# RMSNorm and QKV product on one core: the head of the kernel rewritten as a list schedule, with x tiles first, single weight blocks, and one PSUM pool

## The chip, the cores and the metric

One core of a Trainium2 chip (trn2). The metric is the device time of one execution in microseconds (us); several executions of each kernel are taken and the median is quoted. The profile's span runs from the first to the last instruction and is about 1.8 us shorter than the time. Times inside a profile are counted from the start of the span.

"PE" is the matrix engine, "PEld" its weight loads, "DVE" VectorE, "ACT" ScalarE, "POOL" GpSimd; "SPq" is the queue from which nearly all transfers are issued. In this kernel PE writes its results to tiles in PSUM (eight banks), and VectorE or ScalarE copies them out. A "K block" is 128 of the 768 rows of the weights, and a "unit" is one tile of x times 512 (at the end 256) weight columns.

## The reference

```python
# x: (8, 1024, 768) f32, gamma: (768,), w_qkv: (768, 2304) f32, eps = 1e-5
rms = np.sqrt(np.mean(x ** 2, axis=-1, keepdims=True) + eps)
return np.matmul(x / rms * gamma, w_qkv).astype(np.float32)
```

## The kernel before

The 8192 rows are 64 tiles of 128 rows. A tile of x is transposed (K to the partitions), multiplied with the weights in bf16 (6 K blocks, 4.5 units of 512 columns), and scaled by 1/rms when it is copied out of PSUM. Gamma goes into the weights as they are cast to bf16. The weights are needed whole by every tile and take 7.1 MB, so the kernel begins with a "head": six tiles of x are worked on while the weights arrive in pieces. The 58 other tiles come after it, one after another, and are transposed by transfers instead of by PE.

The order of arrival (w is the next weight piece, x the next tile), and the pieces (first and last K block, first column, columns):

```python
ARRIVALS = "wxxxwxwwxwxww"
PIECES = [(0, 3, 0, 512), (3, 6, 0, 512), (0, 3, 512, 512), (3, 6, 512, 512),
          (0, 6, 1024, 512), (0, 6, 1536, 512), (0, 6, 2048, 256)]
EARLY = 3        # x tiles transposed by PE in f32
FIRST_XBAR = 6   # from this tile on: transposed by a transfer
WARM = 7
...
    psum_t = ctx.enter_context(tc.tile_pool(name="psum_t", bufs=2, space=bass.MemoryType.PSUM))
    psum_mm = ctx.enter_context(tc.tile_pool(name="psum_mm", bufs=6, space=bass.MemoryType.PSUM))
```

Every operation is given a planned time with `at`; at the end the plan is sorted by it and issued. The times only fix the order on each engine; each engine then runs its own list strictly in that order and waits where it must. In the head a simple rule makes the plan: a clock `now` advances with each arrival, casts go to an engine by K block, and each new piece is multiplied with all tiles there are (shortened; the loads, and four more warm-up matmuls behind the transposes of x0, are left out).

```python
    def conv_w(c):
        k0, k1, n0, n = PIECES[c]
        for ko in range(k0, k1):
            ...
            if ko % 3 == 0:   # VectorE   o = i * g
            elif ko % 3 == 1: # ScalarE
            else:             # GpSimd

    at(0.0, idle, WARM)       # matmuls on zeros: keep PE busy
    at(3.0, gamma_in)
    at(3.1, idle, WARM)
    for n, kind in enumerate(ARRIVALS):
        if kind == "x":
            now += 1.02
            if t < EARLY:
                at(now, trans_f32, t); at(now + 0.6, copy_f32, t); ready = now + 1.2
            else:
                at(now, cast_x, t); at(now + 0.6, trans_pe, t); at(now + 1.0, copy_xT, t); ready = now + 1.7
            at(now + 0.7, stat, t)      # ScalarE: sum of squares, root
            at(now + 1.6, recip, t)     # VectorE: waits for stat
            for c in ws: unit(...)      # products with all pieces there are
        else:
            at(now, conv_w, c)
            for t in xs: unit(...)
    for t in range(HEAD, MT):           # the 58 tiles after the head
        at(T - 15, load_x, t); at(T - 8.5, cast_x, t); at(T - 7.5, trans_dma, t)
        at(T - 5, stat, t); at(T - 3, recip, t)
        ...
```

Of the kernel before, what the change touches and what calls it, by code (L numbers as in the profile page):

```python
# [7 lines left out]



ARRIVALS = "wxxxwxwwxwxww"
PIECES = [(0, 3, 0, 512), (3, 6, 0, 512), (0, 3, 512, 512), (3, 6, 512, 512),
          (0, 6, 1024, 512), (0, 6, 1536, 512), (0, 6, 2048, 256)]

EARLY = 3

FIRST_XBAR = 6
WARM = 7


@with_exitstack
def kernel(
# [8 lines left out]
    nc = tc.nc  # L31
    f32 = mybir.dt.float32
    bf16 = mybir.dt.bfloat16
    AF = mybir.ActivationFunctionType
    mult = mybir.AluOpType.mult
# [4 lines left out]
    Kw, N = w_qkv.shape  # L40
    assert K == Kw
    P = 128
    KO = K // P
    MT = M // P
    NT = 512
    HEAD = ARRIVALS.count("x")
    inv_k = 1.0 / float(K)
    PIECE_BUFS = {(k1 - k0, n): sum((q[1] - q[0], q[3]) == (k1 - k0, n) for q in PIECES)
                  for k0, k1, _, n in PIECES}

    PARTS = [(0, 1024), (1024, 1024), (2048, N - 2048)]

    singles = ctx.enter_context(tc.tile_pool(name="singles", bufs=1))
# [4 lines left out]
    xbp = ctx.enter_context(tc.tile_pool(name="xbp", bufs=4))  # L58
    xTp = ctx.enter_context(tc.tile_pool(name="xTp", bufs=HEAD + 3))
    outp = ctx.enter_context(tc.tile_pool(name="outp", bufs=7))  # L60
    psum_t = ctx.enter_context(tc.tile_pool(name="psum_t", bufs=2, space=bass.MemoryType.PSUM))
    psum_mm = ctx.enter_context(tc.tile_pool(name="psum_mm", bufs=6, space=bass.MemoryType.PSUM))

    ctx.enter_context(tc.manual_schedule())

    g6 = singles.tile([KO, P], f32)
    nc.scalar.dma_start(out=g6, in_=gamma.rearrange("(ko p) -> ko p", p=P))
    eps_sb = singles.tile([P, 1], f32)
    nc.vector.memset(eps_sb, float(eps))  # L69
    warm = singles.tile([P, NT], bf16)  # L70
    nc.vector.memset(warm, 0.0)  # L71

    tbl = singles.tile([P, 1], f32)
    nc.scalar.activation(out=tbl, in_=eps_sb, func=AF.Sqrt)  # L74
    ident_f = singles.tile([P, P], f32)
# [3 lines left out]
    g_sb = singles.tile([P, KO], f32)  # L79
    w_b = singles.tile([P, KO, N], bf16)  # L80
    wv = w_qkv.rearrange("(ko p) n -> p ko n", p=P)

    X, XB, XT, RS, OUT, WF, PM, PT = {}, {}, {}, {}, {}, {}, {}, {}
# [5 lines left out]
    def load_w(c):  # L89
        k0, k1, n0, n = PIECES[c]  # L90
        WF[c] = wst.tile([P, k1 - k0, n], f32, name=f"w_f{k1 - k0}_{n}", bufs=PIECE_BUFS[k1 - k0, n])
        nc.sync.dma_start(out=WF[c], in_=wv[:, k0:k1, n0:n0 + n])

    def conv_w(c):
        k0, k1, n0, n = PIECES[c]
        for ko in range(k0, k1):
            o, i, g = w_b[:, ko, n0:n0 + n], WF[c][:, ko - k0, :], g_sb[:, ko:ko + 1]
            if ko % 3 == 0:
                nc.vector.tensor_scalar(out=o, in0=i, scalar1=g, scalar2=None, op0=mult)  # L99
            elif ko % 3 == 1:  # L100
                nc.scalar.activation(out=o, in_=i, func=AF.Copy, scale=g, bias=0.0)  # L101
            else:
                nc.gpsimd.tensor_scalar(out=o, in0=i, scalar1=g, scalar2=1.0, op0=mult, op1=mult)  # L103

    def cast_x(t):
        XB[t] = xbp.tile([P, K], bf16, name="xb")
        nc.vector.tensor_copy(out=XB[t], in_=X[t])  # L107

    def stat(t):
        sq = junk.tile([P, K], bf16, name="sq")  # L110
# [8 lines left out]
        nc.vector.reciprocal(out=r, in_=RS[t])  # L119
        RS[t] = r  # L120

    def trans_pe(t):
        PT[t] = psum_t.tile([P, KO, P], bf16, name="pt")
        for ko in range(KO):
            nc.tensor.transpose(out=PT[t][:, ko, :], in_=XB[t][:, ko * P:(ko + 1) * P], identity=ident)  # L125

    def copy_xT(t):
        XT[t] = xTp.tile([P, KO, P], bf16, name="xT")
        nc.vector.tensor_copy(out=XT[t], in_=PT[t])  # L129

    KA = 4

    def trans_f32(t):
        PT[t] = (psum_t.tile([P, KA, P], f32, name="pt"), psum_t.tile([P, KO - KA, P], f32, name="pt"))
        for ko in range(KO):
            o = PT[t][0][:, ko, :] if ko < KA else PT[t][1][:, ko - KA, :]
            nc.tensor.transpose(out=o, in_=X[t][:, ko * P:(ko + 1) * P], identity=ident_f)  # L137

    def copy_f32(t):
        XT[t] = xTp.tile([P, KO, P], bf16, name="xT")  # L140
        nc.vector.tensor_copy(out=XT[t][:, :KA, :], in_=PT[t][0])  # L141
        nc.scalar.copy(out=XT[t][:, KA:, :], in_=PT[t][1])  # L142

    def trans_dma(t):
        XT[t] = xTp.tile([P, KO, P], bf16, name="xT")
        nc.sync.dma_start_transpose(out=XT[t], in_=XB[t])

    def mm(t, n0, nl, k0=0, k1=KO):
        if k0 == 0:
            PM[t, n0] = psum_mm.tile([P, NT], f32, name="pm")  # L150
        for ko in range(k0, k1):
            nc.tensor.matmul(out=PM[t, n0][:, :nl], lhsT=XT[t][:, ko, :], rhs=w_b[:, ko, n0:n0 + nl],  # L152
                             start=(ko == 0), stop=(ko == KO - 1))

    def part(n0):
        return max(i for i, (p0, _) in enumerate(PARTS) if p0 <= n0)

    def evac(t, n0, nl, on_dve):
        h = part(n0)
        if (t, h) not in OUT:  # L160
            OUT[t, h] = outp.tile([P, PARTS[h][1]], f32, name=f"ot{h}")
        o = OUT[t, h][:, n0 - PARTS[h][0]:n0 - PARTS[h][0] + nl]
        pm = PM[t, n0]
        if on_dve:
            nc.vector.tensor_scalar(out=o, in0=pm[:, :nl], scalar1=RS[t], scalar2=None, op0=mult)  # L165
        else:
            nc.scalar.activation(out=o, in_=pm[:, :nl], func=AF.Copy, scale=RS[t], bias=0.0)  # L167
# [9 lines left out]
    def at(time, fn, *args):  # L177
        plan.append((time, len(plan), fn, args))

    def gamma_in():  # L180
        g_ps = psum_t.tile([P, KO], f32, name="pt")
        nc.tensor.transpose(out=g_ps, in_=g6, identity=ident_f[:KO, :KO])  # L182
        nc.vector.tensor_copy(out=g_sb, in_=g_ps)

    US = 6 * 0.2158 / 512
    left = {}
    state = {"pe": 0.0, "flip": 0}

    def unit(t, n0, nl, ready=0.0, k0=0, k1=KO):
        s = max(state["pe"], ready)  # L190
        state["pe"] = e = s + nl * US * (k1 - k0) / KO
        at(s, mm, t, n0, nl, k0, k1)
        if k1 < KO:
            return
        state["flip"] ^= 1
        at(e + 0.2, evac, t, n0, nl, state["flip"])
        h = part(n0)
        left[t, h] = left.get((t, h), PARTS[h][1]) - nl
        if t == MT - 1:
            at(e + 0.9, store, t, h, n0, nl)  # L200
        elif left[t, h] == 0:
            at(e + 1.4, store, t, h, *PARTS[h])

    def idle(n):
        wps = psum_mm.tile([P, NT], f32, name="pm")
        for _ in range(n):
            nc.tensor.matmul(out=wps, lhsT=warm[:, :P], rhs=warm, start=True, stop=True)  # L207

    at(0.0, idle, WARM)
    at(3.0, gamma_in)  # L210
    at(3.1, idle, WARM)
    now, xs, ws = 2.75, [], []
    for n, kind in enumerate(ARRIVALS):
        if kind == "x":
            t = len(xs)
            at(0.1 * n - 9, load_x, t)
            now += 1.02
            if t < EARLY:
                at(now, trans_f32, t)
                at(now + 0.6, copy_f32, t)  # L220
                if t == 0:
                    at(now + 0.1, idle, 4)
                ready = now + 1.2
            else:
                at(now, cast_x, t)
                at(now + 0.6, trans_pe, t)
                at(now + 1.0, copy_xT, t)
                ready = now + 1.7
            at(now + 0.7, stat, t)
            at(now + 1.6, recip, t)  # L230
            xs.append(t)
            for c in ws:
                k0, k1, n0, nl = PIECES[c]
                unit(t, n0, nl, ready, k0, k1)
        else:
            c = len(ws)
            k0, k1, n0, nl = PIECES[c]
            at(0.1 * n - 9, load_w, c)
            now += (k1 - k0) * nl * 4.1 / (KO * 512)
            at(now, conv_w, c)  # L240
            ws.append(c)
            for t in xs:
                unit(t, n0, nl, now + 0.9, k0, k1)

    n_tiles = [(i, min(NT, N - i)) for i in range(0, N, NT)]
    for t in range(HEAD, MT):
        T = state["pe"]
        at(T - 15, load_x, t)
        if t < FIRST_XBAR:
            at(T - 4.5, cast_x, t)  # L250
            at(T - 3.0, trans_pe, t)
            at(T - 2.5, copy_xT, t)
        else:
            at(T - 8.5, cast_x, t)
            at(T - 7.5, trans_dma, t)
        at(T - 5, stat, t)
        at(T - 3, recip, t)
        for n0, nl in n_tiles:
            unit(t, n0, nl)

    for _, _, fn, args in sorted(plan, key=lambda p: p[:2]):
        fn(*args)
# [35 lines left out]
```

## Time and profile before

| | |
|---|---|
| time, median of 3 runs | 391.52 us |
| span of the profiled run (a run of 392.31 us) | 390.5 us |
| busy: PE, ACT, DVE, POOL | 98%, 47%, 39%, 2% |
| first product of the head | 9.46 us |
| last copy of the head's outputs | 47.89 us |
| last copy of all | 386.89 us |

Read the order of time as: start, length, engine, line of the kernel, operation, output<-inputs, how many; in brackets how long the engine was idle just before, and what ended that.

### The profile page before, as it was taken

The page shows a single profiled execution, that of the slowest core. Times are in us where ns is not written, and L with a number is a line of the kernel's source. Part 1 is how long each engine was busy: PE and PEld are TensorE (multiplying, and loading weights), DVE is VectorE, ACT ScalarE, POOL GpSimd, SP SyncE. Part 2 cuts the span into 40 slices and gives each one's busy share as a digit, 9 for nine tenths or more (in the row PEclk, how much of TensorE's full clock was granted, in tenths as well). Part 3 has the DMA queues.
Part 4 walks back from the last instruction along what each step waited for, and adds up shares of the span by engine and source line. Part 5 has one row for each costly group of instructions (what it writes and reads, how often), then busy time and mean ns, then how long its engine had stood idle before and what let it go on. Part 6 is the DMA issues. An engine that isn't in the chain of part 4 may idle for free.

```text
span 390.5 us, 5469 instructions
## 1 busy us (share of the span) xinstructions
PE 382.4 (98%) x1937; PEld 192.7 (49%) x1975; DVE 152.6 (39%) x305; ACT 182.8 (47%) x367; POOL 7.5 (2%) x16
## 2 busy tenths in 40 slices
PE   8999999999999999999999999999999999999996
PEld 4444644545545545545545545545545545544553
DVE  1564333434333443333443333443334343334332
ACT  3854444444444445444445444435444435444532
POOL 1230000000000000000000000000000000000000
PEclk9999999999999999999999999999999999999999
DMA  8997999999999999999999999999999999999974
GB/s 294 390 387 294 343 267 350 321 342 289 312 308 303 304 264 344 303 309 304 298 314 294 297 316 302 297 318 293 309 311 298 300 297 319 299 323 289 282 268 188
DMA packets 87542, 119.51 MB, mean 306 GB/s; under 512 B 50646, under 2 KB 59612, under 8 KB 87516
## 3 DMA queue, kind: packets, MB, share of 16 engines
q1 hardware_dynamic: 87504, 119.17, 99.9%
q8 instruction: 15, 0.25, 0.3%
q14 instruction: 11, 0.09, 0.1%
q10 hardware_dynamic: 12, 0.00, 0.0%
HBM read 32.25 MB, written 75.50 MB: 276 GB/s over the span
## 4 chain that ended last, share of the span: by engine, by line
PE 95%; DMA 2%; ACT 1%; issue 1%; DVE 0%
PE pm L152 93%; DMA xT<-xb 2%; PE pm L207 2%; ACT sq L112 1%; PE pt L125 0%; ACT xT L142 0%; ACT rms L114 0%; PE pt L137 0%; DVE w_b L99 0%; ACT ot L167 0%; DVE warm L71 0%; PE pt L182 0%; DVE eps_sb L69 0%; DVE rstd L119 0%
## 5 line engine op out<-in xcount | busy, mean ns | idle before, releaser
L152 PE MATMUL pm<-w_b,xT 128*128 128x512 bf16 (+1 forms) x1882 | 372.9, 357 | 3.2 <-DVE xT L141 0.4
L152 PEld LDWEIGHTS <-xT 128*128 128x128 bf16 x1920 | 187.3, 98 | 186.9 <-DVE xT L141 0.9
L165 DVE TENSOR_SCALAR ot<-pm,rstd 128x512 f32<-128x512 f32 (+1 forms) x160 | 111.6, 697 | 220.8 <-PE pm L152 220.7
L167 ACT ACTIVATE ot<-pm,rstd 128x512 f32<-128x512 f32 (+1 forms) x160 | 103.1, 644 | 196.5 <-PE pm L152 151.1
L112 ACT ACTIVATE sq<-x_t 128x768 bf16<-128x768 f32 x64 | 53.3, 834 | 0.0
L107 DVE CAST xb<-x_t 128x768 bf16<-128x768 f32 x61 | 33.1, 543 | 0.5 <-DMA x_t<-in_x_dram 0.5
L114 ACT ACTIVATE rms<-ssq,eps_sb 128x1 f32<-128x1 f32 x64 | 18.9, 295 | 2.1
L112 ACT ACTIVATION_READ_ACCUMULATOR sq<-x_t 128x1 f32 x64 | 12.3, 192 | 0.0
L119 DVE RECIPROCAL rstd<-rms 128x1 f32<-128x1 f32 x64 | 9.8, 154 | 2.5 <-ACT rms L114 2.5
L207 PE MATMUL pm<-warm 128*128 128x512 bf16 x18 | 7.1, 560 | 1.2 <-DVE warm L71 1.2
L101 ACT ACTIVATE w_b<-w_f,g_sb 128x512 bf16<-128x512 f32 (+1 forms) x10 | 6.4, 668 | 2.6 <-DMA w_f<-in_w_qkv_dram 2.6
L103 POOL TENSOR_SCALAR w_b<-w_f,g_sb 128x512 bf16<-128x512 f32 (+1 forms) x10 | 6.8, 690 | 21.8 <-DMA w_f<-in_w_qkv_dram 21.8
L99 DVE TENSOR_SCALAR w_b<-w_f,g_sb 128x512 bf16<-128x512 f32 (+1 forms) x10 | 4.3, 466 | 0.6 <-DMA w_f<-in_w_qkv_dram 0.6
L207 PEld LDWEIGHTS <-warm 128*128 128x128 bf16 x18 | 2.2, 131 | 4.2 <-issue 2.7
L129 DVE COPY xT<-pt 128x768 bf16<-128x768 bf16 x3 | 1.7, 558 | 3.9 <-PE pt L125 3.9
L141 DVE CAST xT<-pt 128x512 bf16<-128x512 f32 x3 | 2.0, 679 | 2.0 <-PE pt L137 2.0
L137 PEld LDWEIGHTS pt<-ident_f,x_t 128*128 128x128 f32 x18 | 2.1, 142 | 0.9 <-ACT xT L142 0.3
L137 PE MATMUL pt<-ident_f,x_t 128*128 128x128 f32 x18 | 2.5, 274 | 0.0
L142 ACT CAST xT<-pt 128x256 bf16<-128x256 f32 x3 | 1.1, 366 | 2.0 <-PE pt L137 2.0
L74 ACT ACT_TABLE_LOAD x1 | 1.3, 1283 | 1.4 <-PEq L279 1.4
L125 PEld LDWEIGHTS <-xb 128*128 128x128 bf16 x18 | 1.2, 98 | 1.0 <-DVE xb L107 0.5
L125 PE MATMUL pt<-ident,xb 128*128 128x128 bf16 x18 | 1.5, 220 | 0.0
(13 smaller groups left out, 2.3 us busy)
## 6 DMA issues: line engine op xcount, KB each, us to landing
out_dram<-ot SPq DMA_DIRECT2D x126, 512.0 KB, 3.8
x_t<-in_x_dram SPq DMA_DIRECT2D x64, 384.0 KB, 4.3
out_dram<-ot SPq DMA_DIRECT2D x64, 128.0 KB, 3.1
w_f<-in_w_qkv_dram SPq DMA_DIRECT2D x5, 768.0 KB, 8.4
w_f<-in_w_qkv_dram SPq DMA_DIRECT2D x2, 1536.0 KB, 14.7
out_dram<-ot SPq DMA_DIRECT2D x4, 256.0 KB, 2.0
xT<-xb SPq DMA_TRANSPOSE x58, 4.4
g<-in_gamma_dram ACTq DMA_DIRECT2D x1, 3.0 KB
```

The lines of the kernel that those rows point to most:

```text
L99: nc.vector.tensor_scalar(out=o, in0=i, scalar1=g, scalar2=None, op0=mult)
L101: nc.scalar.activation(out=o, in_=i, func=AF.Copy, scale=g, bias=0.0)
L103: nc.gpsimd.tensor_scalar(out=o, in0=i, scalar1=g, scalar2=1.0, op0=mult, op1=mult)
L107: nc.vector.tensor_copy(out=XB[t], in_=X[t])
L112: nc.scalar.activation(out=sq, in_=X[t], func=AF.Square, accum_out=ssq)
L114: nc.scalar.activation(out=rms, in_=ssq, func=AF.Sqrt, scale=inv_k, bias=eps_sb)
L119: nc.vector.reciprocal(out=r, in_=RS[t])
L137: nc.tensor.transpose(out=o, in_=X[t][:, ko * P:(ko + 1) * P], identity=ident_f)
L152: nc.tensor.matmul(out=PM[t, n0][:, :nl], lhsT=XT[t][:, ko, :], rhs=w_b[:, ko, n0:n0 + nl], start=(ko == 0), stop=(ko == KO - 1))
L165: nc.vector.tensor_scalar(out=o, in0=pm[:, :nl], scalar1=RS[t], scalar2=None, op0=mult)
L167: nc.scalar.activation(out=o, in_=pm[:, :nl], func=AF.Copy, scale=RS[t], bias=0.0)
L207: nc.tensor.matmul(out=wps, lhsT=warm[:, :P], rhs=warm, start=True, stop=True)
```

## The change

The intent is to let PE work on products sooner and without gaps while the weights arrive. Three tiles of x come first; the first 512 weight columns come as six single K blocks, so that products can follow each block as it lands; a list schedule, worked out beforehand with durations and landing times, fixes the order of everything in the head and chooses an engine for each cast and copy; all eight PSUM banks are one pool. The warm-up matmuls have 128 columns instead of 512. After the head only `FIRST_XBAR` goes, which had no effect with six tiles in the head.

```diff
-ARRIVALS = "wxxxwxwwxwxww"
-PIECES = [(0, 3, 0, 512), (3, 6, 0, 512), (0, 3, 512, 512), ...]
+ARRIVALS = "xxxwwwxwwwwwxxwww"
+PIECES = [(0, 1, 0, 512), (1, 2, 0, 512), (2, 3, 0, 512), (3, 4, 0, 512), (4, 5, 0, 512), (5, 6, 0, 512), (0, 3, 512, 512), ...]
+HEAD_PLAN = [
+    (4.41, "trA", 0), (4.45, "stat", 0), (5.28, "trB", 0), (5.42, "cpA", 0, "DVE"),
+    (5.71, "trA", 1), (5.85, "cpB", 0, "ACT"), (6.10, "recip", 0), (6.44, "stat", 2),
+    ...
+    (7.77, "cpA", 2, "ACT"), (7.81, "conv", 1, 1, "DVE"), (8.02, "mm", 0, 0, "0"), ...
+    (44.67, "evac", 5, 2048, "DVE"),
+]
+HEAD_END = 44.51
-    psum_t = ... bufs=2 ...
-    psum_mm = ... bufs=6 ...
+    psum = ctx.enter_context(tc.tile_pool(name="psum", bufs=8, space=bass.MemoryType.PSUM))
-    def conv_w(c):            # engine by ko % 3
+    def conv(c, ko, eng):     # engine from the plan
-    at(0.0, idle, WARM)
-    at(3.1, idle, WARM)
+    at(0.0, idle, 30)         # 30 of 128 columns
+    for time, op, *args in HEAD_PLAN:
+        ...
+        at(time, ops[op], *args)
```

(cut: four 512-column warm-ups behind the transposes of x0, in place of which five of 128 columns stand behind those of x2; and the rest of the plan, in which the first three tiles are transposed in two parts, "A" with four K blocks and "B" with two, and products name the K blocks they take)

## The prediction

> **What bounds the kernel now.** I read the page's first part, then the waits of the PE, then the order of time of the first 15 us, then stretches of 2.5 us around the end of the head (the six row tiles computed while the weights arrive).
>
> ```profile
> PE 382.4 (98%) x1937; PEld 192.7 (49%) x1975; DVE 152.6 (39%) x305; ACT 182.8 (47%) x367; POOL 7.5 (2%) x16
> ...
> PE 95%; DMA 2%; ACT 1%; issue 1%; DVE 0%
> ...
> L152 PE MATMUL pm<-w_b,xT 128*128 128x512 bf16 (+1 forms) x1882 | 372.9, 357 | 3.2 <-DVE xT L141 0.4
> ```
>
> The PE is the bound: the chain that ended last is 95% PE. The product needs 64 row tiles x 6 K blocks x (4 x 512 + 256) columns. Outputs of consecutive 512-column units are copied out 1.295 us apart (34.89, 37.48 and 40.07 us on VectorE, every second unit), those of 256-column units 0.655 us apart, so a tile costs 4 x 1.295 + 0.655 = 5.83 us and 64 tiles 373.4 us. The span is 390.5, so 17 us are not product. Where are they? The PE's waits:
>
> ```profile
> PE pm L207 <- DVE warm L71: 1.2, 1, 1.2
> PE pm L152 <- DVE xT L141: 0.4, 1, 0.4
> PE pm L152 <- DMA xT<-xb: 0.4, 1, 0.4
> PE pm L152 <- DVE w_b L99: 0.4, 1, 0.4
> ```
>
> Only 1.2 us of real waiting after the warm-up; the rest of the loss is PE time spent on things other than the product (matmuls on zeros, transposes), and the tail. In order of time, engine PE:
>
> ```profile
> 4.52 2.93 PE L207 MATMUL pm<-warm 128*128 128x512 bf16 x7
> 7.29 0.82 PE L137 MATMUL pt<-ident_f,x_t 128*128 128x128 f32 x6
> 7.94 1.03 PE L207 MATMUL pm<-warm 128*128 128x512 bf16 x4
> 8.80 0.82 PE L137 MATMUL pt<-ident_f,x_t 128*128 128x128 f32 x6
> 9.46 0.81 PE L152 MATMUL pm<-w_b,xT 128*128 128x512 bf16 x3
> 10.11 0.85 PE L137 MATMUL pt<-ident_f,x_t 128*128 128x128 f32 x6
> ...
> 13.24 1.46 PE L152 MATMUL pm<-w_b,xT 128*128 128x512 bf16 x5 [0.39 <-DVE w_b L99]
> ```
>
> The first product starts at 9.46 us, and until 13.24 only three threes of them are done: the first weight piece (3 K blocks, 768 KB) comes before the x tiles, whose transposes then trickle in. The last output of the head is copied at:
>
> ```profile
> 47.89 0.47 ACT L167 ACTIVATE ot<-pm,rstd 128x256 f32<-128x256 f32 x1 [0.84 <-PE pm L152]
> ```
>
> From there to the last copy of all (386.89 us) are 339.0 us for 58 tiles, against 58 x 5.83 = 338.4 plus the 0.4 us wait for a transposed tile: the rest is dense, and the change leaves its order alone. So the gain is what the head's end moves, less what comes back as waits behind it. The stretches behind the head (columns: stretch, length, then PE, PEld, DVE, ACT, POOL busy; clock; share of the DMA engines' time; GB/s):
>
> ```profile
> 32.50:35.00 2.50, 2.45 (x12) 1.17 (x12) 0.66 (x2) 0.69 (x1) 0.00 (x0) 1.00 0.65 264
> 35.00:37.50 2.50, 2.50 (x14) 1.09 (x13) 0.66 (x2) 0.69 (x1) 0.00 (x0) 1.00 0.41 163
> 37.50:40.00 2.50, 2.50 (x13) 1.18 (x12) 1.20 (x2) 0.69 (x1) 0.00 (x0) 1.00 0.98 333
> ...
> 50.00:52.50 2.50, 2.50 (x14) 1.14 (x12) 1.29 (x3) 0.69 (x1) 0.00 (x0) 1.00 1.21 221
> ```
>
> The DMA engines are full to 32 us, have 2.5 x 0.35 + 2.5 x 0.59 = 2.35 us of slack in 32.5 to 37.5, and are full again to about 70 us. That slack is what an earlier head uses up.
>
> **What the Trainium skill says.** "TensorE: Matmul & The Clock Gate", section "Wait — 56ns, not 53.3ns?": a 512-column bf16 matmul follows the last after 215.7 ns with the clock warm and 426.7 ns cold. The trace agrees: 1.295/6 = 215.8 ns, and 2.93 us for 7 warm-ups, 0.42 each. Its section "What's actually happening" says that about 3.4 us of sustained work release the clock, in windows that run free of the kernel's start; here the warm-ups from 1.22 us are still spaced by 0.43 at 6.6 us and the four at 7.94 us take 1.03 together, warm. "PSUM — Partial Sum Buffer", section "Specifications (TRN2)", gives 8 banks; both kernels use all eight, 2 + 6 before and one pool of 8 after. "DMA: Bandwidth & Descriptors", section "Specifications", states an HBM limit per core of about 358 GB/s; the trace moves 383 to 401 GB/s in each 5 us stretch from 5 to 30 us, so I use 0.39 MB per us.
>
> **The change, part by part.**
>
> (1) Order of arrival. The first transfer of 768 KB was issued at 0.74 and landed 4.6 us later, 5.34; the x tiles (384 KB) landed 6.25, 7.27 and 8.24, so about 1.0 us each, and 768 KB takes 2.0. The stream thus begins at 5.34 - 2.0 = 3.35. With x first: x0 at 4.35, x1 5.35, x2 6.35, the single K blocks (256 KB, 0.66 each) at 7.0, 7.7, 8.3, x3 9.3, blocks 3 to 5 at 10.0, 10.7, 11.3, the half pieces of columns 512 to 1023 at 13.3 and 15.3, x4 and x5 at 16.3 and 17.3, the whole pieces at 21.4, 25.4, 27.5. Total bytes are unchanged. Each transfer waits for the one eight before it, so smaller pieces mean fewer bytes in flight; but block 5, for instance, waits for x1 (5.35) and is not due on the wires until 10.7: no bubble.
>
> (2) First product. Block 0 at 7.0 plus one POOL cast (0.69 to 0.97 us in the trace; 0.97 when it ran beside a VectorE cast) gives 7.8 to 8.0 instead of 9.46. All three x tiles are transposed by then (f32 transposes are 0.82 per tile; PSUM copies 0.68 and 0.37). The warm-up shrinks to 30 matmuls of 128 columns, about a quarter of 0.43 = 0.107 us each, 3.2 us, ending near 4.4 just as x0 lands.
>
> (3) Density. From 8.0: six tiles x 5.83 = 35.0 us, bf16 transposes of x3, x4, x5 at 0.34 each (the chain's figure) = 1.0. Gaps: PE has 9 block products (1.95 us) for blocks 0 to 2 and is then through at about 10.0; the x3 transposes fill to 10.4; block 3 needs landing 10.0 + VectorE 0.49 plus its latency, 10.6, a gap of 0.2 to 0.3. Blocks 4 and 5 (VectorE 11.2, ACT 12.1) come ahead of their use. The half piece at 13.3 and three casts side by side (0.49, 0.71, 0.69 to 0.97) against PE done at 13.9: 0.1 to 0.3. Later pieces lead by over 1 us. Head end: 8.0 + 35.0 + 1.0 + 0.6 = 44.6, against 47.89. The schedule in the change writes 44.67 for that last copy, a planned time and no measurement, but my sum from the trace lands beside it. PE side gain: 3.2 us. I allow 0.3 of slippage, as an in-order schedule with no slack turns each late cast into a gap: 2.9.
>
> (4) Freedom of engines. VectorE, ACT and POOL do the same 30 casts, redistributed (POOL has 6 of 30, not 10). Over the span none is above 47%, but from 10 to 15 us ACT is busy 4.54 of 5 us, so there its casts count (block 5 at 12.1 above).
>
> (5) One PSUM pool. Walking allocations round robin over 8, each reused bank was copied out 2 us or more before: no wait, and no gain in the steady part, which had none to lose (no PE wait on PSUM above).
>
> (6) What comes back. Loads, six stores of 512 KB and the next x tile are 9.4 + 3.1 + 0.4 = 12.9 MB; at 0.39 per us from 3.35 the DMA is busy to 36. The stores of columns 1024 to 2047 begin after the copy of the first 1536 unit: 38.26 before, near 35.1 after. So the 2.35 us of slack vanish, and the DMA is full from 3.35 to 70 us. In the kernel before, the transposed tile 8 (issued 53.59, landed 6.3 later, 59.9) already came 0.4 us after PE wanted it; tile 7 landed at 47.45 + 5.8 = 53.25 against a start at 53.5, tile 10 at 64.28 + 7.2 = 71.5 against 71.6. With the same transfers in nearly the same order and no idle left, these can come earlier by 2.35 us at most. Whatever the head gains beyond that, PE waits for at tiles 7 to 10. So the gain is about 2.3.
>
> **Sum:** 391.5 - 2.3 = 389.2 us, 0.6% less.
>
> **Rivals.** A: the DMA absorbs the earlier head without extra waits, because some of its share over 1.0 is queueing and not throughput. For: its share counts overlapping packets, and GB/s sinks to 221 where transposes run. Then 2.9 to 3.2 come through: 388.3 to 388.6. B: worse, the full DMA delays both tile 7 and tile 8, or the x tile load now falling among the stores (36.09 before, ahead of them) costs its 1.0 us: gain 1.3, so 390.2. C: the clock is not released by 8.0 us, as the x transposes leave holes between 4.4 and 8: at half clock, up to 3 us of products lose 1.5 us, partly inside the gaps counted: gain 1.2, 390.3. Against it: the PE is busy nearly all the time from 1.1 to 8. D: the small blocks arrive more slowly than the large pieces, or POOL's first cast meets VectorE and takes 0.97: 0.2 to 0.5 us more.
>
> **Range and chances.** Best 388.3 (A), expected 389.2, B or C 390.3; 8 in 10: 388.2 to 390.4. 2% would need 383.7, below even a head without any loss (8 us saved at the start is not to be had when x0 lands at 4.35), so faster by 2% has 0.01, slower by 2% (399.4) needs a fault in the order I did not see, 0.01.
>
> **What would show it.** First product at 7.8 to 8.1; last head copy at 44.6 to 45.0; DMA share near 1.0 in 32 to 37 us; PE waits on transposed tiles rising from 0.4 to about 1 us in all, between 50 and 70 us. If that wait stays 0.4, A holds and I was too low on the gain. A last head copy later than 45.5 with products spaced 0.43 after 8 us would be C. Tail and dense part (386.89 - 47.89 = 339.0 before) should be 339.0 plus the extra wait.

## The result

| | before | after |
|---|---|---|
| time, median of 4 runs | 391.61 us | 389.61 us |
| range of the runs | 391.51 to 391.81 | 389.38 to 389.72 |
| ratio of the fast runs, 95% interval | | 0.9947 (0.993 to 0.9965) |
| span of the profiled run | 390.5 us | 387.9 us |
| last copy of the head's outputs | 47.89 us | 45.33 us |
| last copy of all | 386.89 us | 384.37 us |

A ratio is the mean time of one kernel's fast runs over that of the other's fast runs of the same rounds, so it is not quite the ratio of the medians. The interval excludes 1, so the gain of 2.0 us is real.

The changed kernel's waits of PE:

```profile
PE pm L265 <- DVE eps_sb L124: 1.0, 1, 1.0
PE pm L197 <- DMA x_t<-in_x_dram: 0.8, 1, 0.8
PE pm L216 <- DMA xT<-xb: 0.4, 1, 0.4
PE pm L216 <- POOL w_b L155: 0.4, 1, 0.4
PE pm L216 <- DVE w_b L151: 0.2, 1, 0.2
```

and its order of time, PE with two VectorE lines:

```profile
6.94 0.88 PE L197 MATMUL pm<-ident_f,x_t 128*128 128x128 f32 x6 [0.80 <-DMA x_t<-in_x_dram]
8.48 2.10 PE L216 MATMUL pm<-w_b,xT 128*128 128x512 bf16 x8 [0.39 <-POOL w_b L155]
...
9.90 0.56 DVE L159 CAST xb<-x_t 128x768 bf16<-128x768 f32 x1 [0.51 <-DMA x_t<-in_x_dram]
...
10.52 0.51 PE L183 MATMUL pm<-ident,xb 128*128 128x128 bf16 x6
10.64 0.49 DVE L151 TENSOR_SCALAR w_b<-w_f,g_sb 128x512 bf16<-128x512 f32 x1 [0.18 <-DMA w_f<-in_w_qkv_dram]
11.19 6.80 PE L216 MATMUL pm<-w_b,xT 128*128 128x512 bf16 x30 [0.15 <-DVE w_b L151]
```

The third x tile lands at 6.9 us and PE waits 0.80 for it; block 0 is cast by POOL and the first product starts at 8.48. The nine products of blocks 0 to 2 end at about 10.4, the transposes of x3 fill some of the time, and then everything hangs on weight block 3: landed 10.64, cast 0.49, products from 11.19. The chain that ended last says the same; it goes back through the cast at 10.64 to the transfer of that block, not to the first product. The tile x3 stands only just behind it: it landed at 9.90, VectorE had to cast it first, and in the other profiles of the changed kernel's order (e2, e5, e6, e9, e10, e12) the cast of block 3 follows that cast after 0.66 to 0.68 us without a wait for its own transfer. From 11.19 on PE has no gap worth naming until the head's end.

Why the blocks are late shows in the DMA. First the kernel before, then the changed one, in stretches of 1 us (the last two columns are the DMA's share and GB/s):

```profile
5.00:6.00 1.00, 1.00 (x4) 0.38 (x3) 0.49 (x1) 0.60 (x1) 0.51 (x1) 1.00 1.05 409
6.00:7.00 1.00, 1.00 (x3) 0.30 (x2) 0.00 (x0) 0.12 (x1) 0.46 (x1) 1.00 1.03 412
```

```profile
5.00:6.00 1.00, 1.00 (x9) 0.88 (x9) 0.85 (x4) 0.48 (x2) 0.00 (x0) 1.00 0.90 224
6.00:7.00 1.00, 0.20 (x3) 0.07 (x2) 0.98 (x2) 0.09 (x1) 0.00 (x0) 1.00 0.90 320
```

The changed kernel moves 409 + 412 - 224 - 320 = 277 KB less in these two us, 0.7 us of transfer. It had been ahead before: 46 + 252 + 396 = 694 KB in 1 to 4 us against 16 + 140 + 389 = 545. At 7 us it is 151 KB behind, 0.4 us. The trace has single packets in the dip that took 0.3 to 1.4 us, against 84 to 121 ns for most.

Behind the head, the last copies of tiles 5, 6, 7 (changed kernel) and 6, 7, 8 (before) show where a tile was late. An undisturbed tile takes 5.83 us:

```profile
45.33 0.48 DVE L230 TENSOR_SCALAR ot<-pm,rstd 128x256 f32<-128x256 f32 x1 [0.17 <-PE pm L216]
...
51.16 0.48 DVE L230 TENSOR_SCALAR ot<-pm,rstd 128x256 f32<-128x256 f32 x1 [0.73 <-PE pm L216]
...
57.61 0.47 ACT L232 ACTIVATE ot<-pm,rstd 128x256 f32<-128x256 f32 x1 [1.26 <-PE pm L216]
```

```profile
53.72 0.48 DVE L165 TENSOR_SCALAR ot<-pm,rstd 128x256 f32<-128x256 f32 x1 [1.20 <-PE pm L152]
...
59.56 0.47 ACT L167 ACTIVATE ot<-pm,rstd 128x256 f32<-128x256 f32 x1 [1.26 <-PE pm L152]
...
65.97 0.48 DVE L165 TENSOR_SCALAR ot<-pm,rstd 128x256 f32<-128x256 f32 x1 [1.20 <-PE pm L152]
```

After: 45.33, 51.16 (5.83), 57.61 (6.45): tile 7 came 0.62 late. Before: 59.56 to 65.97 is 6.41: tile 8 came 0.58 late. The wait that the view of waits names (0.4) is a part of this. Everything else behind the head is equal to a few hundredths in every trace, so each span can be written as

span = head end + lateness + 338.43 + tail,

where the lateness is summed over the tiles in this way, 338.43 is the rest of the 58 tiles (e1 and e4, in which no tile was late, have just that), and the tail after the last copy is 3.4 to 4.0 us. For the first pair: 47.89 + 0.58 + 338.43 + 3.61 = 390.5 and 45.33 + 0.62 + 338.43 + 3.54 = 387.9 (rounded). The experiments below are read with this sum. It resolves 0.1 us, but only for the one run that was profiled; repeated times spread by 0.3 to 1.5 us and more.

### The profile page after: what moved, and what is told of

It is laid out like the page before. It is cut to its first block, busy times and chain, and to the rows that moved or that the text cites. A ratio compares the mean times of both kernels' runs of the same rounds, so it can differ in the third digit from the quotient of the medians.

```text
span 387.9 us, 5500 instructions
## 1 busy us (share of the span) xinstructions
PE 379.5 (98%) x1953; PEld 194.3 (50%) x1992; DVE 159.1 (41%) x317; ACT 178.1 (46%) x359; POOL 5.9 (2%) x12
## 4 chain that ended last, share of the span: by engine, by line
PE 94%; DMA 3%; SPq 1%; issue 1%; DVE 0%; ACT 0%
PE pm L216 94%; DMA w_f<-in_w_qkv_dram 2%; DMA xT<-xb 2%; SPq L140 0%; SPq L145 0%; PE pm L183 0%; DVE w_b L151 0%; ACT ot L232 0%; DVE ot L230 0%
## 5 line engine op out<-in xcount | busy, mean ns | idle before, releaser
L230 DVE TENSOR_SCALAR ot<-pm,rstd 128x512 f32<-128x512 f32 (+1 forms) x168 | 116.7, 696 | 210.3 <-PE pm L216 210.3
L232 ACT ACTIVATE ot<-pm,rstd 128x512 f32<-128x512 f32 (+1 forms) x152 | 97.9, 645 | 187.0 <-PE pm L216 141.7
L151 DVE TENSOR_SCALAR w_b<-w_f,g_sb 128x512 bf16<-128x512 f32 (+1 forms) x14 | 6.5, 494 | 6.1 <-DMA w_f<-in_w_qkv_dram 6.0
L155 POOL TENSOR_SCALAR w_b<-w_f,g_sb 128x512 bf16<-128x512 f32 (+1 forms) x6 | 5.2, 864 | 23.5 <-DMA w_f<-in_w_qkv_dram 23.5
L265 PE MATMUL pm<-warm 128*128 128x128 bf16 x35 | 3.8, 300 | 1.0 <-DVE eps_sb L124 1.0
L197 PE MATMUL pm<-ident_f,x_t 128*128 128x128 f32 x18 | 2.8, 292 | 0.8 <-DMA x_t<-in_x_dram 0.8
L197 PEld LDWEIGHTS pm<-ident_f,x_t 128*128 128x128 f32 x18 | 2.2, 155 | 1.1 <-DMA x_t<-in_x_dram 1.0
L159 DVE CAST xT<-pm 128x512 bf16<-128x512 f32 (+1 forms) x3 | 1.7, 596 | 0.0
L159 DVE COPY xT<-pm 128x768 bf16<-128x768 bf16 x3 | 1.6, 547 | 0.0
L183 PE MATMUL pm<-ident,xb 128*128 128x128 bf16 x18 | 1.5, 220 | 0.0
```

What stands on the lines that cost most here:

```text
L151: nc.vector.tensor_scalar(out=o, in0=i, scalar1=g, scalar2=None, op0=mult)
L155: nc.gpsimd.tensor_scalar(out=o, in0=i, scalar1=g, scalar2=1.0, op0=mult, op1=mult)
L159: nc.vector.tensor_copy(out=out, in_=in_)
L197: nc.tensor.transpose(out=PT[t, h][:, ko - k0, :], in_=X[t][:, ko * P:(ko + 1) * P], identity=ident_f)
L230: nc.vector.tensor_scalar(out=o, in0=pm[:, :nl], scalar1=RS[t], scalar2=None, op0=mult)
L232: nc.scalar.activation(out=o, in_=pm[:, :nl], func=AF.Copy, scale=RS[t], bias=0.0)
```

## The experiments

Each call ran on another chip, with its own runs of the kernel before. Runs of one kernel can spread by 1.5 us and more (the unchanged kernel of e2: 388.93 to 390.45), and the changed kernel ran on two of the chips only, so ratios within 0.002 of each other are not told apart by times; the profile's sum is then the better witness, but it is one run. All outputs were correct.

| run | ratio to before (95%) | head end | lateness |
|---|---|---|---|
| before, first profile | | 47.89 | 0.58 |
| after, first profile | 0.9947 (0.993, 0.9965) | 45.33 | 0.62 |
| e1 before again | 1.0007 (0.9988, 1.0025) | 47.54 | 0.00 |
| e2 after again | 0.9947 (0.9933, 0.996) | 45.54 | 0.59 |
| e3 x first | 1.0016 (1.0002, 1.0029) | 48.12 | 0.45 |
| e4 x first, blocks | 0.9996 (0.9984, 1.0009) | 48.83 | 0.00 |
| e5 touch | 0.9973 (0.9956, 0.9989) | 45.40 | 0.67 |
| e6 two pools | 0.9963 (0.995, 0.9976) | 45.34 | 0.64 |
| e7 coarse | 1.0021 (1.0, 1.0042) | 47.88 | 0.37 |
| e8 fixed engines | 0.9965 (0.9953, 0.9978) | 45.51 | 1.39 |
| e9 extra load | 0.9967 (0.9953, 0.998) | 45.44 | 0.80 |
| e10 early transposes | 0.9957 (0.9944, 0.9969) | 45.42 | 0.61 |
| e11 w0 first | 0.9965 (0.9952, 0.9977) | 46.42 | 0.61 |
| e12 two x early | 0.9952 (0.9939, 0.9966) | 46.02 | 0.00 |

### The two kernels again (e1, e2)

No edit.

> The kernel before, unchanged. The first profile of it showed a span of 390.5 us in a run of 392.3 us, while its other runs took 391.5 to 391.8. If the head's end in the profile (last copy of a head output at 47.89 us) moves with that, this profile shows it nearer 47.4 to 47.6, and the change then gains 2.0 to 2.2 us at the head's end rather than the 2.56 us that the first pair of profiles shows. If it stands again at 47.9, the half microsecond lies elsewhere. Ratio of times: 1.000 within 0.001.

> The changed kernel, unchanged. In its first profile the weights' first packets, in the middle of the stream, took up to 1.4 us each between 5.1 and 5.9 us, the DMA moved 219 to 350 GB/s from 5 to 7 us where it moved 390 to 430 before, and the first product started at 8.48 us instead of 7.9. Theory: the first packets to the weights are slow wherever they come in the stream; then this profile shows the same dip at 5 to 6 us and the first product at 8.3 to 8.6. Rival: it was one run's accident; then no dip, and the first product at 7.8 to 8.0. Time 389.4 to 389.8.

The kernel before again:

```profile
4.52 2.33 PE L207 MATMUL pm<-warm 128*128 128x512 bf16 x7
...
47.54 0.47 ACT L167 ACTIVATE ot<-pm,rstd 128x256 f32<-128x256 f32 x1 [0.84 <-PE pm L152]
```

The second seven warm-up matmuls took 2.33 us here and 2.93 in the first profile: the clock was released earlier. In that kernel PE does these matmuls on zeros before it transposes x0, so all of the start, the first product included, came 0.6 us sooner (8.86 instead of 9.46) and the head ended 0.35 sooner. No tile was late. The first profile of before was thus one of its slower runs (392.31 us, median 391.52), while the profile of after is one of 389.72 us (median 389.61): the profiled spans differ by 2.6 us and the medians by 2.0. e1's profile is of its fastest run (391.38); with it the spans differ by 1.7. The expectation for e1 (47.4 to 47.6) held. In e2 the slow packets at 5.1 to 5.9 us are there again, and the first product again starts at 8.48 us: no accident of one run.

### The order of arrival alone, and with single blocks (e3, e4)

```diff
-ARRIVALS = "wxxxwxwwxwxww"
+ARRIVALS = "xxxwwxwwxwxww"            # e3
+ARRIVALS = "xxxwwwxwwwwwxxwww"        # e4, with the six single blocks in PIECES
-    at(3.1, idle, WARM)
```

> The kernel before with only the order of arrival changed: three x tiles first, then the weight pieces of 3 K blocks as they were, and the second seven warm-up matmuls dropped because x0 now lands at 4 us. Theory of the prediction (order and small blocks both matter, since the first product waits for a whole piece of 768 KB plus one cast): first product near 8.2 to 8.9 landing + 0.7 to 1.0 cast = 9.3 to 9.8, no earlier than before (9.46), but six units instead of three by 12 us; gain 0.3 to 1.0 us. Rival: the order alone is nearly the whole gain: 1.7 or more.

> As the run before, with the single K blocks and the arrival order of the change too, but the old rule for casts (VectorE, ACT, POOL by K block modulo 3), old copies, old unit order and two PSUM pools. Theory: order and blocks give most, 1.2 to 1.8 us of the 2.0; what the list schedule, the free choice of engines and the one pool add is 0.2 to 0.8. Rival: the old unit order and the two transposing PSUM banks stall the transposes at the start, and this is worth under 0.7 us.

e3 is no faster than before, and e4 with all the change's transfers gains nothing either (0.9996). Both expectations were too high (the first product of e3 started at 11.53, not at 9.3 to 9.8); I had thought that order and blocks were most of the gain. The profile of e4 is of its slowest run (392.43); three of its five runs took 391.3 to 391.4, against a median of 391.87 for before. In e4, POOL, VectorE and PE:

```profile
9.30 0.69 POOL L103 TENSOR_SCALAR w_b<-w_f,g_sb 128x512 bf16<-128x512 f32 x1 [7.99 <-DMA w_f<-in_w_qkv_dram]
```

```profile
9.75 0.16 DVE L119 RECIPROCAL rstd<-rms 128x1 f32<-128x1 f32 x1 [1.09 <-ACT rms L114]
9.83 0.67 DVE L141 CAST xT<-pt 128x512 bf16<-128x512 f32 x1
10.41 0.48 DVE L99 TENSOR_SCALAR w_b<-w_f,g_sb 128x512 bf16<-128x512 f32 x1
```

Block 2 lands at 9.30 (that is what POOL waited for), so block 0, two blocks of 0.66 us earlier in the stream, was there at about 8.0; but VectorE casts block 0 only at 10.41. Its list is strictly in order, and the old rule put the reciprocal of tile 1's root ahead, which waits 1.09 us for ScalarE. The first product starts at 10.95. The weights wait for the engines, not the engines for the weights. So an earlier arrival was worth something only together with the list schedule. Which part of the schedule mends it is not shown. Besides the reciprocal, a copy of x2's transpose (0.67 us) stood ahead of the cast, and that copy was late in its turn: both runs kept the four 512-column warm-ups ahead of the transposes of x1 (PE, 5.85 to 7.05 us in e3, to 7.33 in e4), and PE waited 0.46 us for a PSUM tile before those of x2. No run takes one of these away alone.

### Is the slow stretch a first reading of the weights? (e5)

```diff
+    touch = singles.tile([P, P], f32)
+    nc.scalar.dma_start(out=touch, in_=w_qkv[0:P, 0:P])
```

> The changed kernel plus one small transfer (128 rows of 512 bytes of the weights) issued on ACT's queue at the start, into a tile nobody reads. Theory: packets to the weights are slow (up to 1.2 us) the first time that this memory is read; the small transfer takes that in the ramp, so the dip of the DMA rate at 5 to 6 us goes, the first block lands at 7.1 instead of 7.7, the first product starts at 7.8 to 8.0 instead of 8.48, and the time falls by 0.4 to 0.6 us against the changed kernel (ratio to before 0.993 to 0.9938 instead of 0.9947). Rival: slowness comes with switching from x to the weights in mid-stream, not with the first reading; then the dip stays and nothing changes.

The theory fell, as far as 64 KB of the weights can test it. The slow packets are there (0.3 to 1.1 us at 5.4 to 6.2 us), the rate is 272 GB/s in 5 to 6 us, the first product starts at 8.61, and the head ends at 45.40. The times are no better (389.71 to 391.93 over six runs).

### One PSUM pool (e6)

```diff
-    psum = ... bufs=8
+    psum_t = ... bufs=2     # transposes and gamma
+    psum = ... bufs=6       # products
```

> The changed kernel with the PSUM pools of the kernel before: two banks for transposes and gamma, six for products. The prediction counted nothing for the one pool in the dense part; in the head, with two banks, each transposed half must be copied out before the next half but one. Worked through with the copies of 0.68 and 0.37 us: last x2 transposes end at 8.6 instead of 7.8, first product at 8.9 to 9.1; partly hidden because block 3 lands at 10.6 whatever happens: loss 0.1 to 0.5 us. Rival: one pool is worth nothing: 0.0 within 0.1. Dense part the same in both.

As expected PE waits for the copies (0.5 and 0.3 us) and the first product is at 8.73 instead of 8.48. But block 3's products start at 11.21 instead of 11.19, and the head ends at 45.34. The one pool is worth nothing in this profile, and the times cannot show a difference (0.9963, interval overlapping that of the change).

### Single blocks (e7)

```diff
-(0, 1, 0, 512), (1, 2, 0, 512), (2, 3, 0, 512), (3, 4, 0, 512), (4, 5, 0, 512), (5, 6, 0, 512)
+(0, 3, 0, 512), (3, 6, 0, 512)
```

> The changed kernel with two weight pieces of 3 K blocks in place of the six single blocks of the first 512 columns; all else as in the change. Theory: the first product waits for 768 KB: landing 8.9 + cast 0.7 = 9.6 instead of 8.48, and the second piece at 12.0 holds the next stretch: loss 0.9 to 1.4 us, most of the gain. Rival: small pieces cost as much in slower arrival as they save: loss under 0.3 us.

The loss is larger than I expected: head end 47.88, 2.55 us later, and the time back at that of before (1.0021). The first product starts at 10.06 instead of 8.48, which was foreseen within half a microsecond. What was not: PE had waited 2.13 us for it, and then

```profile
9.00:10.00 1.00, 0.00 (x0) 0.00 (x0) 0.98 (x3) 0.91 (x4) 0.93 (x1) 0.96 1.04 402
10.00:11.00 1.00, 0.94 (x2) 0.39 (x3) 0.75 (x2) 0.97 (x3) 0.01 (x1) 0.50 1.05 399
```

the granted clock (third column from the right) was 0.50 from 10 to 13 us; by the 0.96 here and 0.83 in 13 to 14 us it was at half from 9.93 to 13.34. In this profile the wait for the larger piece was paid twice, the second time in products at half speed. But that is not what takes the gain away. Half clock for 3.4 us lowers the mean clock of a run by 0.0044, and by it three of the six runs had the fall (mean clock 0.994, 0.995, 0.991; 392.07, 393.03, 394.54 us). The three others (0.998, 0.998, 1.000) took 391.54, 391.54 and 392.06, still some 2 us more than the 389.6 that the ratio of the change gives for this chip. Why they lost more than the expected 0.9 to 1.4 stays open. Nor does a wait of this length always bring the fall. PE waited longer in e3, and there the clock stayed at 1.00:

```profile
11.53 3.40 PE L152 MATMUL pm<-w_b,xT 128*128 128x512 bf16 x15 [2.32 <-DVE w_b L99]
```

(Two of e3's other four runs have a mean clock of 0.994, so they had it.) The clock records of the traces fit steps of 3.41 us that are counted from the moment at which the clock was released: the falls came after a step in which PE was busy for 1.41 us (e7) and 1.76 us (e11), and in e3, where the emptiest step had 1.82 us, there was none. Three cases are not a rule.

### Free choice of engines (e8)

```diff
     def conv(c, ko, eng):
+        eng = ("DVE", "ACT", "POOL")[ko % 3]
     def cp_half(t, h, eng):
+        eng = "DVE" if h == "A" else "ACT"
```

> The changed kernel with the casts back on the engines of the kernel before (K block modulo 3: VectorE, ACT, POOL) and the PSUM halves back on VectorE and ACT, in the same order of time. Theory of the prediction (free choice counted for nothing): within 0.3 us of the changed kernel. Rival: an ACT cast (0.72 us) behind the statistics and a POOL cast (0.7 to 1.0 us) hold blocks 1, 2, 4 and 5, so that PE waits again: loss 0.5 to 1.2 us.

The first product even starts sooner (8.12, VectorE casts block 0), but ScalarE holds blocks 1 and 4 (PE waits 0.32 and 0.35 us), and the head ends at 45.51, 0.18 later than in the change, although block 3's products started 0.13 earlier (11.06). So the choice of engines as such is worth 0.2 to 0.3 us here; that e4 lacked the order and not the assignment follows only in so far as this holds there too. The lateness of 1.39 us for tile 7 in this profile shows how far that term can swing from run to run.

### What makes tile 7 late? (e9, e10, e12)

e9 adds bytes, e10 asks for the transposes earlier, e12 adds the loads of two tiles ahead of the stores:

```diff
+    at(34.0, load_spare, 0); at(34.1, load_spare, 1)        # e9: 0.79 MB nobody reads
```

```diff
-        at(now - 15, load_x, t); at(now - 8.5, cast, t); at(now - 7.5, trans_dma, t)
+        at(now - 17, load_x, t); at(now - 10.5, cast, t); at(now - 9.5, trans_dma, t)   # e10
```

```diff
+    for t in (HEAD, HEAD + 1):                              # e12, with the casts and
+        at(-7.0 + 0.1 * t, load_x, t)                       # transposes of e10
```

> The changed kernel plus two x tiles (0.79 MB, 2.0 us of the DMA engines) loaded at about 34 us into a tile nobody reads. The changed kernel has some 0.7 us of DMA slack left in 35 to 37.5 us (share 0.73) and PE waited 0.44 us for one transposed tile after the head. Theory of the prediction (the transfers between the head and tile 10 are bound by the DMA, so what fills the slack comes out as a PE wait): the wait rises from 0.44 to 1.3 to 2.2 us, head end unchanged at 45.3 to 45.5, time 0.9 to 1.7 us longer than the changed kernel. Rival A: the DMA absorbs it; wait stays at 0.4 to 0.6 and the time is the same.

> The changed kernel with x load, cast and transfer-transpose of each later tile asked for 2 us earlier (17, 10.5 and 9.5 us ahead of its products instead of 15, 8.5 and 7.5). Theory: the wait behind the head is a matter of how far ahead the transpose stands in the queue, not of total bytes; it is then issued before the stores that now stand in front of it, the wait of 0.44 us goes to 0 to 0.1, and the time falls by 0.3 to 0.5 us. Rival: the DMA is short of time as such; another tile (8 or 10) waits instead, time unchanged within 0.1.

> The changed kernel with the loads of x tiles 6 and 7 put right behind the weights, ahead of the first stores, and casts and transfer-transposes 2 us further ahead as in the run before last. In that run the first transpose still left the queue only at 37.9 us, because tile 6 of x, issued at 28.9 behind six stores, had not landed; the queue is in order, so the stores behind it stood still and the DMA moved 63 GB/s in 37.5 to 40 us; tiles 7 and 8 together then came 0.6 us late, as in the changed kernel. Theory: the late x tile in an in-order queue is the cause, not the bytes; here tile 6 is there by 30 us, the first transpose goes at about 35, the next at 41 to 43, and the tiles behind the head come 0.0 to 0.1 us late instead of 0.6: time 0.4 to 0.6 us under the changed kernel, about 389.2 (ratio to before 0.993 to 0.994). Rival: DMA time itself is short in 35 to 60 us; then a later tile waits and the sum stays at 0.5 to 0.6.

e9: the added 2.0 us of transfers, with the slack in 35 to 37.5 us filled (share 1.03), raise the lateness from 0.62 to 0.80 (0.15 at tile 7, 0.66 at tile 8), while the wait was expected at 1.3 to 2.2; the view of waits has 0.48. Bytes are not what binds. Of the 0.7 us by which this profile's span is longer than that of the change, 0.18 is lateness, 0.11 the head and 0.43 the tail after the last copy, which I can't explain by the edit. The ratio is 0.0020 above that of the change, 0.8 us, just under the 0.9 that was expected, and at the limit of what the times tell apart. e10: the lateness stays, 0.61, and is now all at tile 8 (last copies 51.26, 57.09, 63.53). That looks like the rival (DMA short of time), but its queue and one stretch show another thing:

```profile
37.87 1.97 SPq L206 DMA_TRANSPOSE xT<-xb  x1
```

```profile
37.50:40.00 2.50, 2.50 (x14) 1.08 (x13) 2.50 (x5) 1.01 (x3) 0.00 (x0) 1.00 0.50 63
```

Tile 6's transpose, planned for 35.0, is issued at 37.87, and around it the DMA moves only 63 GB/s. Its x tile stood behind six stores of 512 KB and landed late; the queue is in order, so the stores behind the waiting transpose stood too. In e12 the two x tiles are loaded before those stores:

```profile
35.56 1.32 SPq L206 DMA_TRANSPOSE xT<-xb  x1
```

```profile
37.50:40.00 2.50, 2.45 (x13) 1.14 (x12) 1.41 (x3) 0.00 (x0) 0.00 (x0) 1.00 0.95 308
```

The transpose goes 2.3 us earlier, the DMA is not starved, and no tile is late: 0.00, with the bytes unchanged. The later end of this head (46.02) does not explain it: the transpose of tile 7 landed 5.9 us after its issue at 43.22, at 49.1, some 2.6 us before PE was through with tile 6; in the changed kernel it landed at 45.48 + 6.0 = 51.5, 0.4 us too late. Nor is chance likely, although the kernel before had 0.58 and 0.00 in its two profiles: the nine other profiles of the changed kernel and its variants have 0.37 (e7) or more. So it is shown that the DMA's total time is not what holds these tiles: the same bytes, queued in another order, come in time.

That a late x tile is the cause is shown for e10, against which e12 moves only the two loads. For the changed kernel it is likely but not tried alone: there the cast of tile 6 waited for its x tile until 37.78, and its transpose was issued at 38.37 instead of the planned 37.0; e12 differs from it by the shift of e10 as well.

The time did not follow as far as expected: 0.9952, median 389.44 against 391.33 on its chip. In the profile the head ended at 46.02 because the third x tile landed only at 7.68 us; that run had the longest span of the five (388.0; the others 387.4 to 387.7). Whether e12 is faster than the changed kernel by its 0.6 us, the runs do not settle.

### Block 0 before x (e11)

```diff
-ARRIVALS = "xxxwwwxwwwwwxxwww"
+ARRIVALS = "wxxxwwxwwwwwxxwww"
```

> The changed kernel with only the order of arrival altered: the first single weight block ahead of the three x tiles, all else as it is. The small early reading of the weights (run 5) did not take away the slow packets at 5 to 6 us, so a first reading is not their cause. If they belong to the switch from x rows to weight rows, they stay but hit less; if they come at a fixed time after the start, they hit x tiles. Either way block 0 is cast before the x tiles are transposed, and the first product no longer waits for the last arrival: 7.6 to 8.0 us instead of 8.48. But block 3 lands no earlier (the bytes ahead of it are the same), so theory: the head's end moves by 0 to 0.4 us, because the wait moves to block 3. Rival: the first product sets the head's end; then 0.5 to 0.8 us earlier.

Worse in the profile, and neither expectation fits: first product 9.90, head end 46.42. The slow packets came all the same, now in x (0.3 to 1.3 us, begun at 3.8 to 5.5), PE waited twice for x (1.6 us), and the clock fell to 0.55 in 7 to 8 us and 0.50 in 8 to 10. The profiled run is the only one of the five with a mean clock (0.996) that shows such a fall; the others have 0.998 to 1.000 and took 389.77 to 390.69 us against its 390.79, so the head's end of 46.42 stands for this run alone. So the slow stretch belongs neither to a first reading of the weights nor to the switch from x to weights. In the kernel before, whose first transfer is 768 KB of weights, only one packet is slow between 4 and 8 us. Its cause stays open.

## Why the prediction was right, and where its steps were off

The range held (389.61 in 388.2 to 390.4) and the gain was 2.0 us against 2.3, but that is in part luck. Of the signs that the prediction named, one held: from the last head copy to the last copy of all are 384.37 - 45.33 = 339.04 us. The first product (8.48 against 7.8 to 8.1), the last head copy (45.33 against 44.6 to 45.0), the share of the DMA in 32 to 37 us (1.03, then 0.73, against near 1.0) and the PE's wait for transposed tiles (0.4 against about 1) did not. In the first pair of profiles two misses cancel: the head gained 2.56 us instead of 2.9, and behind it 0.04 came back instead of 0.6. With e1's profile for the kernel before, the head gained 2.21 and 0.62 came back. Which of the two is the usual case, the runs do not settle. By its own steps:

1. **Arrival.** The term that was mis-sized. Block 0 was put at 7.0 and came at 7.74, block 3 at 10.0 and came at 10.64. The step took the rate of the kernel before, 0.39 MB per us, for a stream that starts with other transfers; the measured one dips to 224 GB/s in 5 to 6 us.
2. **First product.** 8.48 instead of 7.8 to 8.0, as a consequence. But the weight that the prediction gave to it is wrong, as it counts the head's end from there: in seven profiles of the changed kernel and its variants (after, e2, e5, e6, e9, e10, e12) the first product lies between 8.48 and 9.28, and the head ends 34.12 to 34.15 us after block 3's products start (11.19 to 45.33, 11.21 to 45.34, 11.90 to 46.02). The start of block 3's products sets the end: e6 moves the first product by 0.25 and the end by 0.01, and e2 has the first product of after (8.48) and both the others 0.21 later. What sets that start is the landing of x3 and of block 3, with VectorE's cast of x3 (0.56 us) ahead of that of the block; no run moved that cast.
3. **Density.** 45.33 - 8.48 = 36.85 us against 35.0 + 1.0 + 0.6 = 36.6: right within 0.25. The head's end was thus 0.7 later than 44.6, of which about 0.6 is the late arrival at block 3. The allowance for slippage (0.3) covered half.
4. **Engines** counted for nothing: 0.2 to 0.3 us (e8), right in size. Not foreseen was how the parts hang together: order of arrival and small blocks without the list schedule gain nothing (e4), the list schedule without the blocks gains nothing (e7).
5. **One pool**, nothing: right (e6).
6. **What comes back.** Lateness behind the head was to rise by about 0.6 us because the DMA has no slack left. It was 0.62 against 0.58 in the first pair, and 0.62 against 0.00 with e1's profile. The size lies within that span, but the reason is refuted: the DMA was not full (share 0.73 in 35 to 37.5 us and 0.66 in 42.5 to 45), 2 us more of transfers raise the lateness by 0.18 (e9), and the same bytes in another order take it away (e12). The order of an in-order queue, with a late x tile in it, is what the runs point to instead. Rival A, that the DMA absorbs the earlier head, was nearer.

Rival C (half clock in the change) did not happen: products are 0.216 us apart from 8.48 on and the granted clock is 1.00; it did happen in the profiles of e7 and e11, where PE waited longer, but not in that of e3, where it waited longest. Rival D (small blocks arrive more slowly) gave the right sign for a part of the loss, but e3 with large pieces and x first has the slow packets too, so block size is not the cause.

## What to carry to other kernels

Find the arrival after which PE never stops again, and count from there: what only moved something before it, such as the first product in e6, did not move the end. An earlier arrival is worth little while the cast stands in an in-order list behind operations that wait for another engine; schedule by when inputs are ready, and put the load that a queued transfer depends on before bulk stores. A wait that starves PE for about 2 us can cost twice, as the clock halved after it in some executions (e7, e11) and not in others (e3): look at the mean clock of every run before a profile is taken for the usual case.

## What the Trainium skill lacked or had wrong

- "TensorE: Matmul & The Clock Gate", "What's actually happening", gives an idle window of about 3.4 us before the clock halves. In e7 it was at 0.50 from 9.93 us on, within a wait of PE of 2.13 us (from 7.9 to 10.06), and in e11 at 0.55 in 7 to 8 us after waits of 0.53 and 1.11 us. Gaps shorter than the page's were enough there; in e3 one of 2.32 us was not, so the length of the gap does not decide alone. Nor does the page say that the granted clock of a profile can be blind at the start: it shows 1.00 in 0 to 5 us of both kernels, while the 512-column warm-ups of the kernel before were 0.43 us apart, half speed.
- The same section says that the moment of release varies with a free-running window. That agrees, and here it was worth time: 0.6 us between two profiles of the kernel before, 0.35 us at its head's end.
- "DMA: Bandwidth & Descriptors", "Specifications", gives about 358 GB/s of HBM per core, half of what it gives for a stack. It is no limit for a core that runs alone, as here: 383 to 401 in stretches of 5 us (before), up to 420 in one of 2.5 us (e12).
- No page I read has the slow packets (up to 1.4 us against 0.08 to 0.12) that come at 4 to 6 us in the changed kernel, e3, e4, e5 and e11, and hardly in the kernel before, which loads 768 KB of weights first (one packet of 0.64 us). Blocks 0 and 3 of the changed kernel landed 0.6 to 0.7 us later than predicted; that these packets are the whole reason is not shown.
